# A decoder layer on one core: a fourth pair of weight blocks by seven products of quarters

## The chip, the core and the metric

The kernel runs on one core of a Trainium2 chip. The core's engines run their own instruction streams beside each other and wait for one another by semaphores: PE (TensorE, matrix products into PSUM), DVE (VectorE), ACT (ScalarE), POOL (GpSimd) and SP (SyncE, which here only starts transfers). Data lie in HBM, and are brought to the core's SBUF by DMA queues; SP's queue and POOL's queue are the two that matter. The metric is the device time of one execution in microseconds (us). The time before is the median of three runs, 1008.59 us (1008.1 to 1008.62).

## The reference, cut to what matters

A decoder layer on 256 tokens of width 2048 with two parallel mixers, all in float32:

```
proj = x @ w_in              # q_lat 4096 | c_kv | attn_gate 2048 | indexer | x_rnn 2048 | rnn_gate 2048 | g_a 2048 | g_b 2048
attn = sparse_attention(q_lat, c_kv, ...)                 # 16 heads, top-64 keys
branch_a = (attn * silu(attn_gate)) @ w_branch_a          # 2048 x 2048
h = rglru(x_rnn, ...)       # conv, gates r and i; a = exp(-8 r softplus), b = sqrt(1 - a^2) (i xc); h_t = a h_(t-1) + b
branch_b = (h * silu(rnn_gate)) @ w_branch_b              # 2048 x 2048
merged = sigmoid(g_a) * branch_a + sigmoid(g_b) * branch_b
out = layernorm(2 ** 0.25 * x + merged @ w_out)
```

The change touches how g_a (its first 1024 columns) is computed and when the exponentials and roots of the recurrence are done.

## The kernel before

**Products.** Every float32 value is split into a high and a low part: `hi_of` (L146, ACT) copies the rounded high part, `lo_of` (L150, DVE) subtracts it from the value. A product is three matmuls: high with high, high with low, low with high. The tokens `xs` stay in SBUF in this form. The weights stream: `load_to` has SP fetch pieces of 512 KB into four `raw` buffers, `split_to` turns each into one of five `hi` and five `lo` buffers, and PE uses them. The list `halves` fixes the order of all pieces. `split_to(n + 5)` and `load_to(n + 9)` at the point where PE uses piece n say how far ahead ACT, DVE and SP have been programmed; a buffer is written only when PE (or DVE, for `raw`) is through with what was in it.

**Jobs.** `col_jobs` lists the work in order: qi, the attention gate ag, the latent queries q with the heads beside them, then ga0, ga1, the four blocks of branch A ba0 to ba3, then xr (input of the recurrence), gb1, gb2, rg (its gate), and a tail of branch B and the output product, whose order is a table, and a layer norm. The column tiles of w_in (qi, ag, q, xr, rg) take weights as the stationary operand and are called pairs, in `pair` (two tiles of 128 columns at a time, 32 matmuls of 512 columns and 32 of 256; L384). The blocks of 512 columns (ga, ba, gb, bb) are **chunks**: eight pieces, sixteen ticks, each tick six matmuls 128x512 (two token halves times three, L1310 to L1312), 96 in all.

**Seven products.** Where two blocks multiply the same tokens, their two times two quarters can be had from seven products of quarters in place of eight, with sums of token quarters and of weight quarters. This is done for three pairs: ga2 with gb3 (steps j1 to j4, during q), ga3 with gb0 (steps s1 and s2, `seven_step`, during ba1 to ba3) and bb0 with bb1 (steps t1 to t3, in the tail). The sums of weights for j and s are formed by DVE just before the split; those for t are built in HBM scratch ahead of time by `weight_sums`: SP copies one quarter, POOL starts an accumulating transfer of the other (`add_rows`, L270). The token sums for j are built once during q (`early_sums`, `late_sum`), those for s once more by `quarter_sums`, with loads of x, DVE sums (L990 to L993) and splits, from the start of ga0. An s2 step takes two pieces: one of 1024 columns and one of 512, whose sum (`form`, L368) DVE forms first, and nine matmuls.

**Everything else** hangs on ticks. `spawn(t, generator)` puts a piece of work into an agenda, and `tick(t)` runs each up to its next yield, so a tick decides where in the engines' queues an instruction stands. `D0`, `C0` and `G0` are the ticks where q, xr and the first gb after xr begin. The recurrence: for each of 16 tiles n, `decay(n)` does tanh and exp on ACT (L896, L897), a square on POOL (L900) and a combination on DVE (L902), one tile every four thirds of a tick from G0 + 14; `roots(q)` takes the square roots of four tiles at a time on ACT (L906), G0 + 37 and 38; `post_rg` follows each tile of rg with the eviction (L467, L471), the gate (L920), the scan (L922) and the split of the result.

Of the kernel before, what the change touches and what calls it, by code (L numbers as in the profile page):

```python
# [18 lines left out]
P = 128  # L19
# [35 lines left out]
def col_jobs():  # L55
# [26 lines left out]
YAT = 66  # L82
NAT = 74
# [17 lines left out]
OPERANDS = {"t1a": ("11", "t1"), "t1b": ("t2", "t3"), "t2": ("21", "t4")}  # L101
# [17 lines left out]
def layer(ctx, tc, ar, out):  # L119
# [87 lines left out]
    relb = const.tile([P, P], F32, name="relb")  # L207
# [9 lines left out]
    for job in jobs:  # L217
# [1449 lines left out]
```

## Time and profile before

| what | before |
|---|---|
| median of three runs | 1008.59 us (1008.1 to 1008.62) |
| the profiled execution's own time | 1009.1 us |
| its span, first to last instruction | 1007.3 us |
| mean granted TensorE clock | 0.998 |
| busy: PE / DVE / ACT / POOL | 999.9 / 811.2 / 613.7 / 161.7 us |
| moved by DMA | 233.17 MB, 231 GB/s in the mean |

How to read it: the span is taken from one profiled execution, and 1.8 us of its time lie around it. Busy times are per engine; the engines run beside each other. A row such as `L150 DVE TENSOR_TENSOR lo<-raw,hi 128x1024 ... x360 | 429.2, 1201 | 154.0 <-ACT hi L146 150.2` says: line 150, on DVE, output lo from raw and hi, partitions by elements, 360 of them, 429.2 us busy in all, 1201 ns the mean of one, the engine idle for 154.0 us just before them, of which 150.2 ended when ACT's hi of line 146 was done. In a timeline a row begins with its start and its duration, and a bracket gives idle time before it. In the table by windows each row gives, for a stretch of the span, its length, the busy time and count on each engine, the clock, the share of the DMA engines' time and the rate.

### The profile page before, as it was taken

The page shows a single profiled execution, that of the slowest core. Times are in us where ns is not written, and L with a number is a line of the kernel's source. Part 1 is how long each engine was busy: PE and PEld are TensorE (multiplying, and loading weights), DVE is VectorE, ACT ScalarE, POOL GpSimd, SP SyncE. Part 2 cuts the span into 40 slices and gives each one's busy share as a digit, 9 for nine tenths or more (in the row PEclk, how much of TensorE's full clock was granted, in tenths as well). Part 3 has the DMA queues.
Part 4 walks back from the last instruction along what each step waited for, and adds up shares of the span by engine and source line. Part 5 has one row for each costly group of instructions (what it writes and reads, how often), then busy time and mean ns, then how long its engine had stood idle before and what let it go on. Part 6 is the DMA issues. An engine that isn't in the chain of part 4 may idle for free.

```text
span 1007.3 us, 15201 instructions
## 1 busy us (share of the span) xinstructions
PE 999.9 (99%) x5296; PEld 862.3 (86%) x5296; DVE 811.2 (81%) x1333; ACT 613.7 (61%) x1043; POOL 161.7 (16%) x194
## 2 busy tenths in 40 slices
PE   9999999999999999999999999999999999999997
PEld 8888888888888888888888888888888888888885
DVE  5678789878789988868888868888669898788587
ACT  5576656666776576576555555555886557665452
POOL 0015621111123311210000000000253320000002
PEclk9999999999999999999999999999999999999999
DMA  9846886766656665788988778888786657888952
GB/s 304 263 146 200 273 317 210 236 222 199 189 157 209 198 195 172 232 248 259 280 268 278 225 243 241 275 238 266 223 234 191 202 171 258 271 282 291 325 185 84
DMA packets 77133, 233.17 MB, mean 231 GB/s; under 512 B 8176, under 2 KB 15216, under 8 KB 75776
## 3 DMA queue, kind: packets, MB, share of 16 engines
q1 hardware_dynamic: 71488, 214.20, 64.6%
q0 software_dynamic: 4848, 17.07, 7.4%
q8 instruction: 42, 0.69, 0.3%
q10 hardware_dynamic: 720, 0.92, 0.3%
q14 instruction: 35, 0.29, 0.1%
HBM read 230.03 MB, written 23.10 MB: 251 GB/s over the span
## 4 chain that ended last, share of the span: by engine, by line
PE 99%; DVE 0%; DVEq 0%; issue 0%
PE ps_q L384 18%; PE ps_ag L384 9%; PE ps_rg L384 9%; PE ps_xr L384 9%; PE ps_ba L1311 3%; PE ps_ba L1312 3%; PE ps_ba L1310 3%; PE psq L384 2%; PE ps_qi L384 2%; PE ps_o L1209 2%; PE ps_o L1206 2%; PE ps_o L1207 2%; PE ps_bb L1206 2%; PE ps_bb L1209 2%; PE ps_bb L1207 2%; PE ps_ga L1310 1%
## 5 line engine op out<-in xcount | busy, mean ns | idle before, releaser
L150 DVE TENSOR_TENSOR lo<-raw,hi 128x1024 fp32r<-128x1024 f32 (+1 forms) x360 | 429.2, 1201 | 154.0 <-ACT hi L146 150.2
L146 ACT ACTIVATE hi<-raw 128x1024 fp32r<-128x1024 f32 (+1 forms) x360 | 360.7, 1018 | 146.1 <-PE ps_q L384 16.8
L384 PE MATMUL ps_q<-xs,hi 128*128 128x512 f32 x512 | 126.9, 391 | 0.0
L384 PEld LDWEIGHTS ps_q<-xs,hi 128*128 128x128 f32 x512 | 94.0, 188 | 18.4
L384 PEld LDWEIGHTS ps_q<-xs,lo 128*128 128x128 f32 x512 | 65.6, 191 | 2.5
L384 PE MATMUL ps_q<-xs,lo 128*128 128x256 f32 x512 | 66.4, 283 | 0.0
L641 POOL TENSOR_TENSOR bias<-bias,mask 128x256 f32<-128x256 f32 (+1 forms) x32 | 32.7, 1041 | 194.3 <-DMA bias<-dz 156.6
L384 PE MATMUL ps_ag<-xs,hi 128*128 128x512 f32 x256 | 60.1, 391 | 0.0
L384 PE MATMUL ps_rg<-xs,hi 128*128 128x512 f32 x256 | 59.5, 390 | 0.0
L384 PE MATMUL ps_xr<-xs,hi 128*128 128x512 f32 x256 | 59.5, 390 | 0.0
L384 PEld LDWEIGHTS ps_xr<-xs,hi 128*128 128x128 f32 x256 | 47.6, 188 | 9.6
L384 PEld LDWEIGHTS ps_rg<-xs,hi 128*128 128x128 f32 x256 | 47.6, 188 | 9.6
L384 PEld LDWEIGHTS ps_ag<-xs,hi 128*128 128x128 f32 x256 | 47.5, 188 | 9.6
L1312 PE MATMUL ps_ba<-hi,ua 128*128 128x512 f32 x128 | 49.8, 389 | 0.0
L1311 PE MATMUL ps_ba<-lo,ua 128*128 128x512 f32 x128 | 49.8, 389 | 0.0
L1310 PE MATMUL ps_ba<-hi,ua 128*128 128x512 f32 x128 | 49.8, 389 | 0.0
L146 ACT ACTIVATE hi<-form 128x512 fp32r<-128x512 f32 x40 | 25.3, 633 | 28.4 <-PE ps_ba L1312 8.7
L1206 PE MATMUL ps_o<-hi,xs 128*128 128x512 f32 x96 | 37.6, 392 | 0.0
L1209 PE MATMUL ps_o<-hi,xs 128*128 128x512 f32 x96 | 37.4, 390 | 0.0
L1207 PE MATMUL ps_o<-lo,xs 128*128 128x512 f32 x96 | 37.4, 389 | 0.0
L384 PE MATMUL ps_ag<-xs,lo 128*128 128x256 f32 x256 | 32.9, 283 | 0.0
L384 PE MATMUL ps_xr<-xs,lo 128*128 128x256 f32 x256 | 32.8, 282 | 0.0
(439 smaller groups left out, 2166.3 us busy)
## 6 DMA issues: line engine op xcount, KB each, us to landing
raw<-in_wt SPq DMA_DIRECT2D x168, 512.0 KB, 4.9
raw<-in_wba SPq DMA_DIRECT2D x32, 512.0 KB, 4.9
raw<-in_wo SPq DMA_DIRECT2D x32, 512.0 KB, 4.6
raw<-in_wga SPq DMA_DIRECT2D x24, 512.0 KB, 4.8
raw<-in_wgb SPq DMA_DIRECT2D x20, 512.0 KB, 5.1
raw<-in_wbb SPq DMA_DIRECT2D x20, 512.0 KB, 4.5
sum_t<-in_wbp SPq DMA_DIRECT2D x16, 512.0 KB, 6.6
raw<-in_ws SPq DMA_DIRECT2D x16, 512.0 KB, 4.7
```

What stands on the lines that cost most here:

```text
L146: nc.scalar.activation(hi, src, AF.Copy)
L150: nc.vector.tensor_sub(lo, src, f(hi))
L384: nc.tensor.matmul(ps[:, :n], w, rhs[:, :n], start=start, stop=stop)
L641: nc.gpsimd.tensor_add(b[:, r, :W[r]], b[:, r, :W[r]], mask[:, r, :W[r]])
L1206: nc.tensor.matmul(o, mh, hi, start=left[t] == left_of[key][t], stop=False)
L1207: nc.tensor.matmul(o, mh, lo, start=False, stop=False)
L1209: nc.tensor.matmul(o, ml, hi, start=False, stop=left[t] == 0)
L1310: nc.tensor.matmul(o, mh, hi, start=first and d == 0, stop=False)
L1311: nc.tensor.matmul(o, mh, lo, start=False, stop=False)
L1312: nc.tensor.matmul(o, ml, hi, start=False, stop=d == KT - 1)
```

## The change

- **A fourth pair.** ga0 and ga1 are no longer chunks. They are computed as the quarters of one product in four kinds of steps, r1 (8 steps), r2 (4), r3 (8), r4 (8), each with one piece and six matmuls 128x512 (`r_step`, L1185 to L1187 after the change), 168 matmuls where there were 192. Their results are combined by `after_r1` to `after_r4`.
- **Its weight sums** are built in HBM scratch like those of t, by the same `weight_sums`, now with a set, from tick 4 on, every 11 ticks with pauses (16 copies by SP, 16 accumulating transfers by POOL).
- **Token sums are stored and fetched again.** `early_sums` and `late_sum` store what they built for j to HBM scratch `kept` (SP, in the q stage). `load_sums`, from the start of gb1, fetches it by 16 transfers on POOL's queue into buffers that the last heads give back; the r and s steps read them. `quarter_sums` is gone. Signs of sums are changed so that the same token sums serve all three pairs.
- **Order.** gb1 moves from behind xr to ahead of the ba chunks; the ba chunks come in the order 2, 0, 1, 3. The table `EXTRAS` says which steps stand ahead of which piece of which chunk. In s2, six steps now stand in a row ahead of the last piece of ba3, where steps and pieces alternated.
- **The recurrence.** tanh is done with each tile's gates in xr. `decays` does eight tiles at once: 0 to 7 at C0 + 50, 8 to 15 at G0 + 17, with the first roots at G0 + 18 and the rest at G0 + 34. Only one chunk, gb2, is left between xr and rg. `lru_consts` comes earlier, and the buffer for `decay` is allocated at C0 and later holds y.

PE, in the middle of the first chunk after q, between heads 13 and 14 of the attention (`ps_ga0_0` and `ps_ga0_1` are the two token halves of ga0; hi and lo are the split pieces by number). Before:

```order
L1310 MATMUL ps_ga0_0_4881<-hi138_4830,xs_93 128x512
L1311 MATMUL ps_ga0_0_4881<-lo138_4831,xs_93 128x512
L1312 MATMUL ps_ga0_0_4881<-hi138_4830,xs_93 128x512
L1310 MATMUL ps_ga0_1_4882<-hi138_4830,xs_93 128x512
L1311 MATMUL ps_ga0_1_4882<-lo138_4831,xs_93 128x512
L1312 MATMUL ps_ga0_1_4882<-hi138_4830,xs_93 128x512
```

The same place after the change (`psr_1` and `psr_2` are two of the seven products, `ps_gb1_0` a token half of gb1):

```order
L1185 MATMUL psr_1_5080<-hi138_4939,xs_93 128x512
L1186 MATMUL psr_1_5080<-lo138_4940,xs_93 128x512
L1187 MATMUL psr_1_5080<-hi138_4939,xs_93 128x512
L1185 MATMUL psr_2_5081<-hi138_4939,xs_93 128x512
L1186 MATMUL psr_2_5081<-lo138_4940,xs_93 128x512
L1187 MATMUL psr_2_5081<-hi138_4939,xs_93 128x512
L1185 MATMUL psr_1_5080<-hi139_4971,xs_93 128x512
L1186 MATMUL psr_1_5080<-lo139_4972,xs_93 128x512
L1187 MATMUL psr_1_5080<-hi139_4971,xs_93 128x512
L1428 MATMUL ps_gb1_0_4989<-hi140_4983,xs_93 128x512
```

A chunk's piece is used for twelve matmuls, a step's piece for six, so the pieces follow each other faster where steps stand.

ACT, where rg begins (`gb2` is evicted, `ri` and `decay` belong to the recurrence, hi268 and hi280 are pieces of rg). Before:

```order
L772 ACTIVATE gb2_0_7998<-ps_gb2_0_7768 128x512
L146 ACTIVATE hi268_8000<-raw268_7894 128x1024
L772 ACTIVATE gb2_1_8017<-ps_gb2_1_7769 128x512
L896 ACTIVATE decay_7743<-ri15_7710,c8_91 128x256
L897 ACTIVATE ri15_7710<-ri15_7710,nc8_92 128x256
L906 ACT_TABLE_LOAD
L906 ACTIVATE decay_7743<-decay_7743 128x1024 x2
L146 ACTIVATE hi269_8059<-raw269_7918 128x1024
L906 ACTIVATE decay_7743<-decay_7743 128x1024 x2
```

After:

```order
L174 ACTIVATE hi280_8093<-raw280_7989 128x1024
L944 ACT_TABLE_LOAD
L944 ACTIVATE ri8_7623<-ri8_7623,nc8_92 128x256
L944 ACTIVATE ri9_7640<-ri9_7640,nc8_92 128x256
L944 ACTIVATE ri10_7792<-ri10_7792,nc8_92 128x256
L944 ACTIVATE ri11_7806<-ri11_7806,nc8_92 128x256
L944 ACTIVATE ri12_7928<-ri12_7928,nc8_92 128x256
L944 ACTIVATE ri13_7946<-ri13_7946,nc8_92 128x256
L944 ACTIVATE ri14_8028<-ri14_8028,nc8_92 128x256
L944 ACTIVATE ri15_8061<-ri15_8061,nc8_92 128x256
L958 ACT_TABLE_LOAD
L958 ACTIVATE decay_6725<-decay_6725 128x1024 x2
```

Eight exponentials, two loads of tables and two roots now stand between two splits; before, the exponentials were spread over the gb chunks.

DVE, behind that place, after the change (a2 are the squares that POOL made, lo280 to lo284 the low parts of rg's pieces, s_rg the evicted tile):

```order
L178 TENSOR_TENSOR lo280_8094<-raw280_7989,hi280_8093 128x1024
L960 MEMSET decay_6725 128x4 x2
L954 SCALAR_TENSOR_TENSOR decay_6725<-a28_8128,decay_6725 128x256
L954 SCALAR_TENSOR_TENSOR decay_6725<-a29_8140,decay_6725 128x256
L954 SCALAR_TENSOR_TENSOR decay_6725<-a210_8152,decay_6725 128x256
L178 TENSOR_TENSOR lo281_8168<-raw281_8007,hi281_8167 128x1024
L954 SCALAR_TENSOR_TENSOR decay_6725<-a211_8164,decay_6725 128x256
L178 TENSOR_TENSOR lo282_8188<-raw282_8035,hi282_8187 128x1024
L954 SCALAR_TENSOR_TENSOR decay_6725<-a212_8182,decay_6725 128x256
L510 TENSOR_TENSOR s_rg0_8205<-ps_rg0_8080,r_rg0_8185 128x256
L178 TENSOR_TENSOR lo283_8208<-raw283_8069,hi283_8207 128x1024
L954 SCALAR_TENSOR_TENSOR decay_6725<-a213_8202,decay_6725 128x256
```

Before, the combinations (L902) were all ahead of rg's second tile; now eight stand among its low parts.

The diff, cut to its core:

```diff
-    jobs += [("ga", i) for i in range(2)] + [("ba", i) for i in range(4)]
+    jobs += [("gb", 1)] + [("ba", i) for i in (2, 0, 1, 3)]
     jobs += [("xr", i) for i in range(16)]
-    jobs += [("gb", i) for i in range(1, 3)] + [("rg", i) for i in range(16)]
+    jobs += [("gb", 2)] + [("rg", i) for i in range(16)]
...
-    return {("ba", 1): ("s1", (0, None, 1, None, 2, None, 3, None)),
-            ("ba", 2): ("s1", (4, None, 5, None, 6, None, 7, None)),
-            ("ba", 3): ("s2", tuple(range(8)))}.get(job)
+    return EXTRAS.get(job, ((),) * 8)
...
+RAT = 4
+RGAP = 11
+RPAUSE = {1: 6, 2: 6, 3: 6, 4: 6, 5: 6, 6: 48}
...
+    ("gb", 1): ((), (), R1[0:2], R1[2:4], (), (), R1[4:7], ()),
+    ("ba", 2): ((), R1[7:8], R3[0:1], R3[1:4], R3[4:5], (), R3[5:8], ()),
+    ("ba", 0): (R4[0:3], R4[3:8], (), (), R2[0:2], R2[2:4] + S1[0:1], S1[1:2], ()),
+    ("ba", 1): (S1[2:3], S1[3:4], (), (), (), (), (), S1[4:5]),
+    ("ba", 3): (S1[5:6], S1[6:7], S1[7:8], (), (), S2[0:1], S2[1:2], S2[2:8]),
...
-    def decay(n):
-        r, w = ri[n][:, :T], v[:, n, :]
-        nc.scalar.activation(w, r, AF.Tanh, scale=c8[:, n:n + 1])
-        nc.scalar.activation(r, r, AF.Exp, scale=nc8[:, n:n + 1])
...
+    def decays(ns):
+        for n in ns:
+            nc.scalar.activation(ri[n][:, :T], ri[n][:, :T], AF.Exp, scale=nc8[:, n:n + 1])
...
+    def load_sums():
...
+            for s, d in zip((2, 3, 1, 4), dst):
+                nc.gpsimd.dma_start(f(d), kept[s, j])
...
+    def r_step(phase, k):
+        i = where[phase, k]
+        split_to(i + 5)
+        load_to(i + 9)
...
+        todo = {"r1": lambda: ((1, a(k, 0)), (2, a(8 + k, 0))),
+                "r2": lambda: ((4, a(8 + 2 * k, 1)), (4, a(9 + 2 * k, 1))),
+                "r3": lambda: ((6, S[2, k]), (7, S[3, k])),
+                "r4": lambda: ((5, S[1, k]), (3, S[4, k]))}[phase]()
...
+            nc.tensor.matmul(psr[p], mh, hi, start=first, stop=False)
+            nc.tensor.matmul(psr[p], mh, lo, start=False, stop=False)
+            nc.tensor.matmul(psr[p], ml, hi, start=False, stop=last)
+        parts.pop(i)
+        split_to(i + 6)
+        load_to(i + 10)
...
-    spawn(C0 + WAT, weight_sums(WGAP))
+    spawn(C0 + WAT, weight_sums("t", WGAP, {}))
+    spawn(RAT, weight_sums("r", RGAP, RPAUSE))
...
-    spawn(at["ga", 0] + 2, quarter_sums())
+    spawn(at["gb", 1] + SAT, load_sums())
...
-    for n in range(16):
-        spawn(G0 + 14 + 4 * n // 3, decay(n))
+    spawn(C0 + DEC, decays(range(8)))
+    spawn(G0 + DEC2, decays(range(8, 16)))
     for q in range(4):
-        spawn(G0 + 37 + q // 2, roots(q))
+        spawn(G0 + (DEC2 + 1, DEC2 + 1, ROOTS, ROOTS)[q], roots(q))
```

More of the change, by code (lines that the diff above doesn't have):

```diff
@@ L113, in ticks @@
 def ticks(job):
-    return 16 if job[0] in CHUNKS else 4
+    if job[0] not in CHUNKS:
+        return 4
+    return 16 + sum(phase[0] == "r" for steps in seven(job) for phase, _ in steps)
 @with_exitstack
@@ L153, in layer @@
     accs, auxs = [0, 1, 2, 3], [4, 5, 6, 7]
+    order = list(range(8))
     def bank(n, name):
+        n = order[n]
         return psum.tile([P, 512], F32, name=name, tag=f"bank{n}", bufs=1)
@@ L221, in layer @@
         for pc in range(8 if job[0] in CHUNKS else 2):
-            step = seven(job) and (seven(job)[0], seven(job)[1][pc])
-            if step and step[1] is not None:
+            for step in seven(job)[pc] if job[0] in CHUNKS else ():
                 where[step] = len(halves)
-                halves += [(step[0] + e, step[1], 0) for e in "ab"]
+                halves += [(step[0] + e, step[1], 0) for e in ("ab" if step[0][0] == "s" else ("",))]
             where[job, pc] = len(halves)
@@ L298, in load_to @@
                 src = ar["ws"][a + (8 if kind == "s2a" else 0)].rearrange("p k c -> p (k c)")
+            elif kind == "r2":
+                for e in range(2):
+                    nc.sync.dma_start(raw[:, e * 512:(e + 1) * 512], quarter("r", "t4", 2 * a + e))
+                continue
             elif kind == "t3":
@@ L770, in post_gb @@
         for t in range(2):
-            g = gates["gb", i, t] = gate_tile(f"gb{i}_{t}", "form")
+            if i == 1:
+                g = att.tile([P, 512], F32, name=f"gbt{t}", tag="gbt", bufs=2)
+            else:
+                g = gate_tile(f"gb{i}_{t}", "form")
+            gates["gb", i, t] = g
             nc.scalar.activation(g, pss[t], AF.Copy)
             yield
+    done = set()
     def post_ba(i, pss):
         for t in range(2):
+            assert i == 3 or (i, t) in done, (i, t)
             g = gates["ga", i, t]
@@ L956, in layer, with load_quarters @@
     S = {}
-    def load_quarters(n):
-        x = [gate_tile(f"form{n}_{j}", "form") for j in range(8)]
+    def load_quarters():
+        x = [gate_tile(f"form0_{j}", "form") for j in range(8)]
         form.update(enumerate(x))
@@ L1026, in early_sums @@
                     SJ[s, 2 * j + e] = (homes[s, j][:, e, 0, :], homes[s, j][:, e, 1, :])
+        yield KEEP
+        for j in range(4):
+            for s in v:
+                nc.sync.dma_start(kept[s, j], f(homes[s, j]).rearrange("p k e t -> p (k e t)"))
+                yield 2
     def late_sum(j):
@@ L1046, in late_sum @@
             SJ[3, 2 * j + i] = (hi[:, i, :], lo[:, i, :])
+        yield 3
+        for e, part in enumerate((hi, lo)):
+            nc.sync.dma_start(kept[3, j][:, e * T:(e + 1) * T], f(part).rearrange("p k t -> p (k t)"))
     psj = {}
@@ L1113, in layer, with after_r2 @@
+    def after_r2():
+        nc.vector.tensor_add(cr["c"], psr[4], cr["c"])
+        accs.insert(1, 3)
+        auxs.append(7)
+        yield
+        for e, n in enumerate("bcad"):
+            nc.scalar.activation(cr[n], cr[n], AF.Sigmoid)
+            done.add(divmod(e, 2))
+            yield
+    after_r = {("r1", 7): after_r1, ("r2", 3): after_r2, ("r3", 7): after_r3, ("r4", 7): after_r4}
     ps7 = {}
@@ L1165, in after_s2 @@
             nc.scalar.activation(g, v, AF.Sigmoid)
+        yield
+        for t in range(2):
+            g = gate_tile(f"gb1_{t}", "form")
+            nc.scalar.activation(g, gates["gb", 1, t], AF.Copy)
+            gates["gb", 1, t] = g
     SB = {}
```

216 lines of the change are left out of this document (137 added, 79 removed).

## The prediction

> **What bounds the kernel now.** I read the page's first two parts, then the waits of PE, then the chain.
>
> ```profile
> PE 999.9 (99%) x5296; PEld 862.3 (86%) x5296; DVE 811.2 (81%) x1333; ACT 613.7 (61%) x1043; POOL 161.7 (16%) x194
> DMA  9846886766656665788988778888786657888952
> GB/s 304 263 146 200 273 317 210 236 222 199 189 157 209 198 195 172 232 248 259 280 268 278 225 243 241 275 238 266 223 234 191 202 171 258 271 282 291 325 185 84
> PE 99%; DVE 0%; DVEq 0%; issue 0%
> ...
> PE warm L397 <- DVE eps L200: 1.0, 1, 1.0
> PE psn L1537 <- ACT mrow L146: 0.4, 1, 0.4
> PE pm L1534 <- DVE mcol L1531: 0.3, 1, 0.3
> ```
>
> The span is 1007.3 us, PE is busy for 999.9 of it, and its three waits together are 1.7 us: one at the start, two in the layer norm at the end. So between them nothing is waited for, and the time is the number of PE instructions times what each takes. A microsecond less on PE is a microsecond less in all, as long as the split pieces (ACT's high part, DVE's low part) and the transfers stay ahead. VectorE at 81% and transfers at eight tenths say that the reserve is not large; so I price PE first and then look for the places where the change eats the reserve.
>
> **What leaves PE.** Gates ga0 and ga1 were two chunks of 96 matmuls. Now they are 28 steps r1 to r4 of 6 matmuls, 168, all of the same shape 128x512.
>
> ```profile
> L1310 PE MATMUL ps_ga<-hi,xs 128*128 128x512 f32 x64 | 25.3, 395 | 0.0
> L1311 PE MATMUL ps_ga<-lo,xs 128*128 128x512 f32 x64 | 24.9, 389 | 0.0
> L1312 PE MATMUL ps_ga<-hi,xs 128*128 128x512 f32 x64 | 25.0, 390 | 0.0
> ...
> core 0: us, PE busy (x) PEld busy (x) DVE busy (x) ACT busy (x) POOL busy (x), PEclk, DMA share, GB/s
> 466.33:488.09 21.76, 21.76 (x97) 18.02 (x96) 18.80 (x29) 12.32 (x19) 1.03 (x1) 1.00 0.93 279
> ```
>
> The three rows are the 192 matmuls of ga0 and ga1. Their 390 ns is the length of one, and neighbours overlap, so the cost of one more or less is read from a stretch of nothing else: chunk ba0, alone from 466.33 to 488.09, is 96 matmuls in 21.76 us at full clock, 0.2267 us each. 24 fewer are **5.44 us** less. Every other product remains: gb1, the ba chunks and s1, s2 are moved and not lengthened, and sign changes turn a subtraction into an addition of the same shape.
>
> The Trainium skill ("TensorE: Matmul & The Clock Gate", section Back-to-back issue gap) gives 131 ns for one in a sustained stream of 512 columns, and 216 ns for an isolated one; by the first the 24 would be worth 3.1 us and the time 1005.8, by the second 5.2 us and 1003.8. The window above shows 226.7 ns in a stream, so neither holds here and the trace's figure is taken.
>
> **What is added beside PE.** Splitting 28 pieces in place of 16 adds 12 times 1.20 us on DVE and 12 times 1.02 us on ACT. Against that go the second set of token sums:
>
> ```profile
> L150 DVE TENSOR_TENSOR lo<-raw,hi 128x1024 fp32r<-128x1024 f32 (+1 forms) x360 | 429.2, 1201 | 154.0 <-ACT hi L146 150.2
> L146 ACT ACTIVATE hi<-raw 128x1024 fp32r<-128x1024 f32 (+1 forms) x360 | 360.7, 1018 | 146.1 <-PE ps_q L384 16.8
> L990 DVE TENSOR_TENSOR sum<-form,form x4: 416/418/421, 445.1 to 472.1; 128x256 f32<-128x256 f32 x4
> form<-in_xT POOLq DMA_DIRECT2D x16, 256.0 KB, 6.2
> ```
>
> L990 (shortest, median and longest in ns) is one of four such lines, 16 sums of 0.42 us with 16 low parts as short (13 us), and 16 high parts on ACT. DVE so gains about 14.4 + 7 combinations of 0.69 us (the form sum's row, below) - 13 = 6 us over a stage of 109 us, ACT about 6: both have more idle than that in the stage (DVE's busy share in ba0 is 18.80 of 21.76, so 15 us per 109). In the mean it is hidden.
>
> The sums come back by 16 transfers of 256 KB on POOL's queue. A row of the same size and queue takes 6.2 us to land. The last group may start only once head 15 (pspv15) is through; r3's fifth and seventh step, the first to read groups that wait so, come 54 and 90 matmuls behind it, 12 and 20 us. That is twice the landing: cost 0, and 3 us at most, if two groups queued one behind the other (2 x 6.2 plus some 2 us of POOL's issues, less 12). Behind the waiting POOL instruction stand only the sums for the tail, needed 250 us later. The 16 copies and 16 accumulating transfers of the weight sums start at tick 4 and are spread over the ag and q stages, where the slices show 146 to 236 GB/s; POOL waits there for copies that are three gaps of 11 ticks old: 0.
>
> **Three places where the reserve could run out.**
>
> (a) Transfers, from gb1 to the end of ba0. PE has 480 matmuls there, 108.8 us. To be moved: 52 pieces of 0.524 MB, two s1 steps of 0.786, 16 returning sums of 0.262, five copies and two accumulations of 0.524 for the tail's sums, one bias: 36.9 MB. Nine pieces (4 raw, 5 split) are there beforehand, 4.7 MB, so 32.2 MB in 108.8 us, **296 GB/s**.
>
> ```profile
> 480.00:520.00 40.00, 40.00 (x178) 33.14 (x177) 34.60 (x42) 20.64 (x24) 3.02 (x3) 1.00 0.89 269
> 120.00:135.00 15.00, 15.00 (x85) 13.18 (x84) 12.75 (x40) 9.37 (x13) 8.36 (x13) 1.00 1.02 385
> 900.00:945.00 45.00, 45.00 (x211) 37.15 (x210) 35.71 (x38) 24.91 (x27) 0.00 (x0) 1.00 0.89 312
> 735.61:746.72 11.11, 11.11 (x66) 9.86 (x65) 6.01 (x9) 9.86 (x14) 4.04 (x5) 1.00 1.02 286
> ```
>
> The last two columns are the share of the 16 engines and the rate. 312 GB/s ran for 45 us at 0.89, 385 for 15 us; but the stretch with accumulating transfers (480 to 520) has 269 at the same 0.89, which is 302 at full share, and one short stretch was full at 286. All four ran without a wait of PE. 296 lies inside; I take 0, with 0 to 13 us as ends (36.9 MB at 302 with no lead is 122 us, for 108.8). At 286 it would be 112.6, a stall of 3.8.
>
> (b) Six steps of s2 in a row at the end of ba3, where before a step and a chunk piece took turns.
>
> ```profile
> L368 DVE TENSOR_TENSOR form<-form,raw 128x512 f32<-128x512 f32 x8 | 5.5, 686 | 0.1
> L150 DVE TENSOR_TENSOR lo<-form,hi 128x512 fp32r<-128x512 f32 x40 | 27.9, 698 | 0.1
> 563.21 0.63 ACT L146 ACTIVATE hi<-form 128x512 fp32r<-128x512 f32 x1 [1.39 <-PE ps_ba L1312]
> ```
>
> A step needs 0.69 + 1.20 + 0.70 = 2.59 us of DVE and 9 matmuls, 2.04 us, of PE. Six in a row leave DVE 3.3 us behind. The last row, from the same stage, shows ACT waiting for PE to free a buffer, so the lead of five buffers is full, two and a half steps or 6.5 us of DVE's work: 0 taken, 0 to 3.3 as ends. Behind the run come pairs of xr, which use fewer pieces per microsecond, and the lead is built again.
>
> (c) The start of rg. Two tables are loaded, eight exponentials and two roots done by ACT in one burst between two splits.
>
> ```profile
> L897 ACT ACTIVATE ri<-ri,nc 128x256 f32<-128x256 f32 x16 | 8.2, 511 | 0.5
> 735.61 88.88 PE ps_rg L384 x512
> 737.33 1.05 ACT L146 ACTIVATE hi<-raw 128x1024 fp32r<-128x1024 f32 x1
> 739.82 1.28 ACT L906 ACT_TABLE_LOAD   x1
> 741.11 2.01 ACT L906 ACTIVATE decay<-decay 128x1024 f32<-128x1024 f32 x2
> 748.48 1.59 DVE L150 TENSOR_TENSOR lo<-raw,hi 128x1024 fp32r<-128x1024 f32 x1 [1.86 <-ACT hi L146]
> 753.20 1.34 DVE L150 TENSOR_TENSOR lo<-raw,hi 128x1024 fp32r<-128x1024 f32 x1 [1.05 <-ACT hi L146]
> 754.91 0.42 ACT L920 ACTIVATE g<-s_rg 128x256 f32<-128x256 f32 x1 [1.74 <-DVE s_rg L471]
> 756.92 1.04 ACT L146 ACTIVATE hi<-raw 128x1024 fp32r<-128x1024 f32 x1
> L902 DVE SCALAR_TENSOR_TENSOR decay<-a,decay 128x256 f32<-128x256 f32 x16 | 8.4, 550 | 0.5 <-POOL a L900 0.5
> ```
>
> The burst is 2 x 1.28 + 8 x 0.51 + 2.01 = 8.7 us. The split before it ended 2.8 us into rg (737.33 + 1.05 - 735.61), so the next ends at 2.8 + 8.7 + 1.06 = 12.5. Two tiles of rg take 88.88/8 = 11.11 us on PE; the buffer that this split writes is freed at 8.3 (four high parts, 7.3, and one low part, 0.95), and PE wants it at 11.11 + 1.83 = 12.94. It is 0.4 us early, by a clock that can be wrong by as much. After that eight combinations of 0.55, 4.4 us, stand between the low parts on DVE, whose idle time there is 1.86 + 1.05 = 2.9; they slip by 1.5, ACT's gate (754.91, waiting for DVE) with them, and the split behind it, which ended at 757.96 and was wanted at 735.61 + 22.22 + 1.83 = 759.66, 1.7 before. Again nearly nothing is left. I take **0.4 us** lost, with 0 and 2.7 as ends (burst and slip each late by their own length over the lead, plus a landing that was waited for 1.15 us). The other eight exponentials, done in one burst during xr, fall where the buffers are full: 0, up to 1.
>
> The Trainium skill ("ScalarE: Activation LUTs", section What ACT_TABLE_LOAD costs) has a drain of 1.38 us behind each load. Here the next instruction starts 0.01 us after the load's end (739.82 + 1.28, 741.11), so the trace disagrees.
>
> **Sum.** On the profiled execution, 1007.3 and 1.8 around it, 1009.1: 1009.1 - 5.44 + 0.4 = 1004.1. The median of the runs shown is 0.5 lower, 1008.59, and gives **1003.5**.
>
> **Rivals.** *The reserve runs out in part*: the burst of (c), the run of (b) or the transfers of (a) at 286 cost 1 to 4 us; 1004.5 to 1006.6. For it: (c) has half a microsecond left by its own working. Against it: PE never waited in places as dense.
> *The drain counts*: each of the two loads holds ACT 1.4 us more, by (c) nearly all of it is late, and PE waits 2.4 us more: 1005.9. The two rows speak against it. It is inside the first rival's range, and I give it 0.03 of its chance. The drain is the rule of the Trainium skill named above ("ScalarE: Activation LUTs").
> *The transfers bound the r stage*: from gb1 to ba0 the rate stays at 302 and the lead was not full, so PE waits 13.4 us, net 8 slower, 1016.6. It decides from 282 GB/s on: there the stall, 32.2 MB in 114.2 us, eats the 5.44; below 277 the kernel is slower by more than 0.2%. For it: 302 at full share with accumulating transfers. Against: 312 and 385 without.
> *The gain is eaten*: (a) and (c) together cost 3.5 to 7.5, within 0.2% of before.
> *The change does not do what it says*: the instructions are counted, 24 fewer on PE, so only if the order made PE wait as much; that is the case just named.
>
> **Chances.** Clean (1002.8 to 1004.3) 0.60; partly run out (to 1006.6) 0.20; within 0.2%, 2.0 us, about what a measurement of this kernel can tell from no change, 0.12; slower 0.08. The range of 8 in 10 leaves out 0.03 below and most of the last two cases: 1002.5 to 1007.0, its upper end being a stall of 3.5 us, in the middle of the ends of (a) to (c).
>
> **What would show it.** PE's instructions fall by 24 and its busy time by 5.4; its list of waits stays at the three rows (clean), or gains one: on ACT's hi or DVE's lo in the second or third pair of rg for (c), in ps (s2) at the end of ba3 for (b), on a transfer (raw or kept) or on hi behind raw between gb1 and ba0 for (a). The rate in that stage should be near 296 (36.9 MB over a somewhat longer stretch when the lead is rebuilt). ACT should show the burst as one row of 8 x 0.51 with the splits late behind it. Wrong would be: waits of PE over 4 us in sum, or matmuls that take other than 0.2267 us beside the denser transfers.

## The result, and the profile after

The changed kernel took 1022.65 us (median of four runs, 1019.25 to 1024.12) against 1008.61 us for the kernel before on the same chip (1008.1 to 1009.16): 1.0134 times the time before, 95% interval 1.0109 to 1.0160. It is 14 us slower, where 5 less were forecast. The profiled execution, the shortest of the four, took 1019.25 us with a span of 1017.4. That is 10.1 us above the profiled execution before, and these are accounted for below; the three longer runs left no trace.

After the change, the page's busy times, transfers by slice and chain, then the list of PE's waits (total, times, longest):

```profile
PE 999.8 (98%) x5272; PEld 858.2 (84%) x5272; DVE 819.8 (81%) x1320; ACT 625.8 (62%) x1046; POOL 182.1 (18%) x218
...
DMA  8759998899868978888998777887858658888952
...
PE 82%; DMA 6%; DVE 5%; ACT 5%; issue 2%; SPq 0%; DVEq 0%; ACTq 0%
...
PE ps_rg L423 <- ACT hi L174: 4.1, 2, 3.7
PE psr L1185 <- issue: 1.6, 1, 1.6
PE psj L1119 <- DVE gb L1147: 1.2, 1, 1.2
PE ps_ba L1429 <- DVE lo L178: 1.2, 1, 1.2
PE ps_ba L1428 <- ACT gbt L815: 1.1, 1, 1.1
```

PE has its 24 instructions less, but the chain, which was PE for 99%, is PE for 82%: it now runs through transfers, DVE and ACT. The three waits of before were 1.7 us; the five new ones shown are 9.2 us, and one loss cannot be seen in this list, a slower clock behind the longest of them (below).

Where the time went is read from the first and last starts of PE's instructions on one tile. Before, then after (shortest, median and longest in ns, then first and last start):

```profile
L1310 PE MATMUL ps_ga<-hi,xs x64: 389/389/481, 416.8 to 465.6; 128*128 128x512 f32 x64
L384 PE MATMUL ps_xr<-xs,hi x256: 388/389/398, 591.6 to 683.5; 128*128 128x512 f32 x128
L384 PE MATMUL ps_rg<-xs,hi x256: 389/389/398, 735.5 to 820.3; 128*128 128x512 f32 x128
```

```profile
L1428 PE MATMUL ps_gb<-hi,xs x64: 389/389/481, 418.8 to 738.3; 128*128 128x512 f32 x64
L423 PE MATMUL ps_xr<-xs,hi x256: 388/389/398, 616.3 to 708.2; 128*128 128x512 f32 x128
L423 PE MATMUL ps_rg<-xs,hi x256: 387/389/628, 738.9 to 830.1; 128*128 128x512 f32 x128
```

From the first chunk behind q to xr (the **r stage**) it was 174.8 us, is 197.5, and should be 191.1: 72 matmuls more stand there (gb1 came, 24 went), 16.3 us. rg's first to last start grew from 84.8 to 91.2, and up to the tail's first matmul from 88.8 to 95.3. In this way each stage of each profile was set against its count of matmuls; us lost, with the medians:

| run | median us | ratio to before, interval | q | r stage | xr | gb2 | rg | start of tail |
|---|---|---|---|---|---|---|---|---|
| the change | 1022.65 | 1.0134 [1.0109, 1.0160] | 1.7 | 6.4 | 0.1 | 0.4 | 6.5 | -0.1 |
| e1_roots | 1015.44 | 1.0067 [1.0052, 1.0082] | 0.9 | 8.7 | 0.1 | 1.6 | 0.1 | 0.0 |
| e2_tsums | 1015.55 | 1.0071 [1.0050, 1.0093] | 1.0 | 1.2 | 0.1 | 0.0 | 4.5 | 0.7 |
| e3_spread | 1024.05 | 1.0147 [1.0128, 1.0165] | 1.5 | 12.1 | 0.1 | 2.1 | 6.1 | -0.1 |
| e4_all | 1012.69 | 1.0041 [1.0025, 1.0058] | 1.5 | 1.7 | 0.0 | 1.7 | 0.9 | 2.8 |
| e5_memset | 1020.32 | 1.0110 [1.0095, 1.0125] | 1.7 | 9.1 | 0.1 | 1.2 | 5.0 | 0.4 |
| e6_nokept | 1016.86 | 1.0083 [1.0068, 1.0098] | 2.1 | 7.2 | 0.1 | 1.4 | 6.0 | 0.0 |
| e7_noaccum | 1012.78 | 1.0036 [1.0022, 1.0050] | 2.3 | 3.9 | 0.0 | 0.0 | 3.0 | 0.4 |
| e8_norsums | 1020.27 | 1.0118 [1.0097, 1.0139] | 0.2 | 8.7 | 0.1 | 0.2 | 7.6 | 0.0 |
| e9_raw5 | 1012.93 | 1.0044 [1.0029, 1.0059] | 1.2 | 1.2 | 0.1 | 0.1 | 5.9 | -0.1 |
| e10_best | 1016.02 | 1.0080 [1.0066, 1.0093] | 1.0 | 3.2 | 4.6 | 4.3 | 0.1 | 0.0 |
| e11_best_s | 1019.72 | 1.0102 [1.0089, 1.0115] | 1.7 | 6.4 | 4.6 | 4.0 | 0.1 | 0.5 |
| e12_queues | 1020.36 | 1.0113 [1.0097, 1.0129] | 1.5 | 8.2 | 0.1 | 1.5 | 5.3 | 0.4 |
| e13_queues_t | 1020.33 | 1.0106 [1.0092, 1.0120] | 1.5 | 4.4 | 0.1 | 0.0 | 6.0 | 4.4 |
| e14_queues_t_r | 1023.89 | 1.0150 [1.0122, 1.0177] | 5.0 | 4.5 | 0.1 | -0.1 | 8.6 | 2.8 |
| e15_roots_t6 | 1010.33 | 1.0020 [1.0010, 1.0030] | 1.2 | 4.7 | 0.2 | 3.1 | 0.1 | 0.0 |
| e16_roots_t | 1013.64 | 1.0045 [1.0031, 1.0060] | 1.6 | 1.9 | 0.1 | 1.6 | 1.3 | 4.4 |

(start of the tail: first matmul of bb2 to first of bb3). For the change the losses come to 15.0, with 0.3 at the kernel's start 15.3; less the 5.44 that left PE, 9.9 of the 10.1 us. A kernel that waits varies more from run to run than the one before; the columns come from one execution each, so a microsecond there, or two in the medians, says little, and a tenth is rounding. Two profiles lie far from their medians: e2's is its shortest run of ten (1011.05 of 1011.05 to 1020.62), e15's one of its longer ones (1012.98).

Part of some columns is a stretch in which PE ran at half its clock (last section), 1.7 us each: in rg of the change, e2, e3, e5, e6, e9 and e13 (2.6 and 2.8 in e8 and e14), in the r stage of e3, e11, e13 and e14, in gb2 of e10, xr of e11, q of e14 and the tail of e13 and e16.

How the r stage waits is seen at the first r4 step. ACT and DVE after the change (start, duration, in brackets the idle time before and what ended it):

```profile
487.07 1.06 ACT L174 ACTIVATE hi<-raw 128x1024 fp32r<-128x1024 f32 x1 [3.02 <-DMA raw<-in_wga]
...
490.32 1.06 ACT L174 ACTIVATE hi<-raw 128x1024 fp32r<-128x1024 f32 x1 [0.72 <-DMA raw<-in_wga]
...
491.41 1.23 DVE L178 TENSOR_TENSOR lo<-raw,hi 128x1024 fp32r<-128x1024 f32 x1 [0.55 <-ACT hi L174]
492.55 0.68 DVE L1201 TENSOR_TENSOR ga<-psr,ga 128x512 f32<-128x512 f32 x1
```

A piece lands late, ACT's high part waits for it, DVE's low part for that, and behind the low part in DVE's queue stands the combination that empties the PSUM bank (L1201, done at 493.23). r4's first matmul, which needs that bank, started at 493.3, 1.8 us late; the list of waits calls it "issue". The wait for `gbt` is the same by way of ACT: the eviction of gb1 stood in its queue behind a split whose piece was late.

At the start of rg, ACT, DVE and POOL after the change, and two windows (PE busy first, then clock):

```profile
744.80 3.31 ACT L944 ACTIVATE ri<-ri,nc 128x256 f32<-128x256 f32 x8
...
749.40 2.01 ACT L958 ACTIVATE decay<-decay 128x1024 f32<-128x1024 f32 x2
...
750.53 0.06 DVE L960 MEMSET decay<- 128x4 f32 x1 [5.79 <-ACT decay L958]
751.46 0.42 DVE L954 SCALAR_TENSOR_TENSOR decay<-a,decay 128x256 f32<-128x256 f32 x1 [0.86 <-POOL decay L966]
...
755.14 0.95 DVE L954 SCALAR_TENSOR_TENSOR decay<-a,decay 128x256 f32<-128x256 f32 x1
756.01 1.63 DVE L178 TENSOR_TENSOR lo<-raw,hi 128x1024 fp32r<-128x1024 f32 x1
...
756.52 1.72 POOL L966 TENSOR_TENSOR decay<-decay,ri 128x256 f32<-128x256 f32 x1
...
764.16 0.42 ACT L972 ACTIVATE g<-s_rg 128x256 f32<-128x256 f32 x1 [3.64 <-DVE s_rg L510]
...
766.48 1.04 ACT L174 ACTIVATE hi<-raw 128x1024 fp32r<-128x1024 f32 x1
...
763.40:767.70 4.30, 0.57 (x3) 0.15 (x3) 4.01 (x8) 1.96 (x4) 4.02 (x6) 1.00 0.39 138
767.70:771.60 3.90, 3.90 (x11) 3.05 (x12) 3.61 (x5) 2.82 (x6) 0.53 (x2) 0.56 0.94 170
```

DVE stands still for 5.8 us behind a memset that waits for ACT's roots. Then the combinations come together with POOL's products, and both get slow: 0.95 us beside POOL where one alone took 0.42, a low part 1.63 for 1.23. The second tile's gate on ACT (764.16) waits 3.6 us for DVE, the split behind it (766.48) ends 22.7 us after the first exponential, PE waits 4.1 us from start to start, and runs at 0.56 of its clock, in the mean, for the 3.9 us after that. The burst of exponentials and roots also began late: the first exponential stood 5.9 us into rg, and 1.25 us of that was ACT's wait for a piece of rg to land.

### The profile page after: what moved, and what is told of

The parts are those of the page before. It is cut to its first block, busy times and chain, and to the rows that moved or that the text cites. A ratio compares the mean times of both kernels' runs of the same rounds, so it can differ in the third digit from the quotient of the medians.

```text
span 1017.4 us, 15291 instructions
## 1 busy us (share of the span) xinstructions
PE 999.8 (98%) x5272; PEld 858.2 (84%) x5272; DVE 819.8 (81%) x1320; ACT 625.8 (62%) x1046; POOL 182.1 (18%) x218
## 4 chain that ended last, share of the span: by engine, by line
PE 82%; DMA 6%; DVE 5%; ACT 5%; issue 2%; SPq 0%; DVEq 0%; ACTq 0%
PE ps_q L423 18%; PE ps_ag L423 9%; PE ps_rg L423 7%; PE ps_xr L423 6%; ACT hi L174 2%; DVE lo L178 2%; PE psq L423 2%; PE ps_qi L423 2%; PE ps_o L1323 2%; PE ps_o L1326 2%; PE ps_o L1324 2%; PE ps_bb L1324 2%; PE ps_bb L1323 2%; PE ps_bb L1326 2%; PE ps_ba L1429 2%; PE ps_ba L1428 2%
## 5 line engine op out<-in xcount | busy, mean ns | idle before, releaser
L178 DVE TENSOR_TENSOR lo<-raw,hi 128x1024 fp32r<-128x1024 f32 (+1 forms) x372 | 441.2, 1196 | 141.6 <-ACT hi L174 138.6
L174 ACT ACTIVATE hi<-raw 128x1024 fp32r<-128x1024 f32 (+1 forms) x372 | 374.2, 1020 | 177.0 <-DMA raw<-in_wt 17.4
L423 PE MATMUL ps_rg<-xs,hi 128*128 128x512 f32 x256 | 61.8, 398 | 4.1 <-ACT hi L174 4.1
```

Of the source, the lines that this page charges most:

```text
L174: nc.scalar.activation(hi, src, AF.Copy)
L178: nc.vector.tensor_sub(lo, src, f(hi))
L423: nc.tensor.matmul(ps[:, :n], w, rhs[:, :n], start=start, stop=stop)
```

## The experiments

All are the changed kernel but for the edit shown, timed against the kernel before. e6 to e9 leave out work that the result needs, and serve for the times alone.

**e1_roots.** The first eight tiles' roots into xr.

```diff
-        spawn(G0 + (DEC2 + 1, DEC2 + 1, ROOTS, ROOTS)[q], roots(q))
+        spawn((C0 + DEC + 10, C0 + DEC + 10, G0 + ROOTS, G0 + ROOTS)[q], roots(q))
```

> The first eight tiles' roots are taken in xr (C0 + 60) in place of the start of rg; nothing else moves. Theory rg-burst (the DVE's memset that waits for the roots holds up eight combinations, and these then run beside POOL's squares and slip behind the splits): the two waits of PE in rg (0.8 and 4.1 us from start to start) and the slow matmuls behind the longer one go, rg takes 89 to 90 us in place of 95.3, and the time falls by 4 to 7 us. Rival (the exponentials and table loads alone make hi late, or the transfers of rg do): rg stays at 93 us or more, time falls by less than 2 us.

Measured: 1015.44 us, 7 below the change; rg lost 0.1 in place of 6.5. PE's row, DVE's behind the eight exponentials, then ACT's:

```profile
L423 PE MATMUL ps_rg<-xs,hi x256: 389/389/398, 740.4 to 825.3; 128*128 128x512 f32 x128
...
746.69 1.16 DVE L954 SCALAR_TENSOR_TENSOR decay<-a,decay 128x256 f32<-128x256 f32 x2 [1.35 <-POOL a L951]
...
749.68 1.33 DVE L178 TENSOR_TENSOR lo<-raw,hi 128x1024 fp32r<-128x1024 f32 x1 [0.51 <-ACT hi L174]
...
745.39 3.31 ACT L944 ACTIVATE ri<-ri,nc 128x256 f32<-128x256 f32 x8
...
761.03 1.05 ACT L174 ACTIVATE hi<-raw 128x1024 fp32r<-128x1024 f32 x1
```

The matmuls run from 740.4 to 825.3, 84.9 us as before the change, and none is over 398 ns. From the first exponential to the end of the split behind the second gate (761.03; the **rg path** below) it is now 16.7 us; in the change, and in the six other runs that leave rg alone (e2, e3, e6 to e9), it is 22.7 to 22.8. So what rg lost came from the roots' place in the burst, and they are worth 6.0 us of that path. With the roots went ACT's 3.3 us for them, the memsets behind them and four products of POOL (L966); what part is whose, this run does not say. gb2, which now follows the roots closely, lost 1.6.

**e2_tsums, e3_spread.** The tail's sums later; the same r steps spread more evenly.

```diff
-WAT = -84
-WGAP = 11
+WAT = 4
+WGAP = 7
```

> The tail's weight sums are built from xr on (16 copies, 16 accumulations, every 7 ticks) in place of from the middle of ba2 on; rg's burst stays. Theory transfers (the stretch from gb1 to ba1 moves too much, so raw pieces land late): with 5 MB less in it, the 6.4 us lost between gb1 and xr shrink to 2 to 4, the time falls by 2 to 4 us, and the waits of ACT for raw pieces there get shorter. Rival crowding (four raw buffers and a landing of 5 us limit the steps in bursts, whatever else is moved): the loss there stays at 5 to 6.5 us. A cost is possible in xr or rg, where the copies go now: up to 2 us.

```diff
-    ("gb", 1): ((), (), R1[0:2], R1[2:4], (), (), R1[4:7], ()),
-    ("ba", 2): ((), R1[7:8], R3[0:1], R3[1:4], R3[4:5], (), R3[5:8], ()),
-    ("ba", 0): (R4[0:3], R4[3:8], (), (), R2[0:2], R2[2:4] + S1[0:1], S1[1:2], ()),
+    ("gb", 1): ((), (), R1[0:2], R1[2:3], R1[3:4], R1[4:5], R1[5:7], ()),
+    ("ba", 2): ((), R1[7:8], R3[0:1], R3[1:3], R3[3:5], R3[5:6], R3[6:8], ()),
+    ("ba", 0): (R4[0:2], R4[2:5], R4[5:8], (), R2[0:2], R2[2:4] + S1[0:1], S1[1:2], ()),
```

> The same steps, spread more evenly: r3 1-2-2-1-2 in place of 1-3-1-0-3, r4 2-3-3 in place of 3-5. Theory crowding: the loss between gb1 and xr shrinks from 6.4 to 2 to 4 us, time lower by 2 to 4 us. Theory transfers (bytes of the whole stretch): the loss stays at 5 to 6.5 us, as the bytes are the same.

Measured: e2 1015.55, the r stage lost 1.2 in place of 6.4; e3 1024.05, the r stage lost 12.1. Spreading the steps inside their chunks helped nothing: the r4 steps still stand in the first half of ba0, so the pieces needed there are the same. Taking the tail's transfers out of the stage helped: e2's 1.2 is from its shortest run, but the other four runs with its `WAT` lost 1.7, 1.9, 4.4 and 4.5 there (e4, e16, e13, e14; 1.7 of each of the last two is half clock), against 6.4 to 12.1 where these sums were built at their old place (the change, e1, e3, e5, e8, e12).

**e4_all.** The three edits together.

> All three moves together. If their causes are separate the gains add: rg 89 to 90 us, the loss between gb1 and xr under 2 us, time 1004 to 1010. If a shared limit stands behind both (transfers everywhere), the sum stays above 1014.

Measured: 1012.69. Both losses went (1.7 and 0.9), but gb2 lost 1.7 and the tail's start 2.8, by one wait:

```profile
PE ps_bb L1324 <- DVE lo L178: 2.5, 1, 2.5
```

The gains of e1 and e2 are 14.3 us together, and e3 cost 1.4; 10 were had.

**e5_memset.** DVE's memset ahead of the root.

```diff
-        nc.scalar.activation(w, w, AF.Sqrt)
-        yield
         nc.vector.memset(w[:, :, 0:1], 1.0)
+        nc.scalar.activation(w, w, AF.Sqrt)
+        yield
```

> In roots the memset of the first token's column stands ahead of the root (the root of 1 is 1) in place of behind it; so DVE's queue no longer waits for ACT's roots at the start of rg. Roots, exponentials and POOL's products stay where the change put them. Theory queue (DVE stood still 5.8 us behind that memset with eight combinations ready behind it): rg takes 89 to 91 us in place of 95.3, the time falls by 4 to 6 us. Rival port (the combinations are slow because POOL runs beside DVE, 0.95 us in place of 0.42) or rival burst (ACT's exponentials, roots and table loads): rg stays at 93 us or more, the time falls by less than 2.

Measured: 1020.32, rg lost 5.0. Here is why so little; DVE, then POOL:

```profile
747.43 1.16 DVE L954 SCALAR_TENSOR_TENSOR decay<-a,decay 128x256 f32<-128x256 f32 x2 [1.33 <-POOL a L951]
753.24 0.95 DVE L954 SCALAR_TENSOR_TENSOR decay<-a,decay 128x256 f32<-128x256 f32 x1 [4.65 <-POOL a L951]
...
751.89 0.74 POOL L966 TENSOR_TENSOR decay<-decay,ri 128x256 f32<-128x256 f32 x1 [3.92 <-ACT decay L959]
```

DVE got past the memset, did two combinations, and then waited 4.65 us for a square that stood in POOL's queue behind a product that needs ACT's roots. The wait had moved to another queue: the rg path took 21.9 us here, 0.8 less than in the change.

**e6_nokept, e7_noaccum.** Without the fetch of the stored sums; without the accumulating transfers of the tail's sums.

```diff
-                nc.gpsimd.dma_start(f(d), kept[s, j])
...
+                    S[s, 2 * j + k] = [xs[:, 2 * j + k, s // 3 * P:s // 3 * P + P], xs[:, 2 * j + k, T:T + P]]
```

> The 16 transfers that bring the stored token sums back (4.2 MB on POOL's queue, in gb1 and ba2) are left out; the r and s steps read slices of xs in their place. Theory bytes (the stretch from gb1 to xr carries too many bytes, of whatever kind): 4.2 MB less bring about what e2's 5 MB less brought, the loss there shrinks from 6.4 to 1.5 to 3 us and the time falls by 4 to 7. Rival (it is the tail's copies and accumulations that hurt, by reading and writing HBM at once): the loss shrinks by 2 us at most, as these still run from ba2 on.

```diff
-                if len(begun) > 2:
+                if len(begun) > 2 and set == "r":
...
-        while begun:
+        while begun and set == "r":
```

> The 16 accumulating transfers of the tail's weight sums are left out, their 16 copies stay at their places. Theory bytes: of what the tail's sums move in the stretch the accumulations are about a third by count (two or three of seven or eight), so the loss there shrinks by 1 to 2.5 us. Theory accumulation (these are what slows the other transfers): it shrinks by 4 us or more, to about what e2 left. Theory copies: no change, within 1 us.

Measured: e6 1016.86, but its profile shows 7.2 lost in the r stage, no better than the change; this one is inconclusive, its median speaking for the theory of bytes and its profile (1019.28, its longest run) against. e7 1012.78, with 3.9 lost there: by these single profiles the accumulations are about half of what e2 removed. e7 also lost only 3.0 in rg. Its rg path took 22.8 us, as in the change, but it began 3.3 us into rg in place of 5.9, and no stretch of half clock followed; so when the burst begins, and with it the landing that ACT waits for ahead of it, is part of rg's loss. The other runs bear this out: the first exponential 4.0 us into rg goes with 4.5 lost (e2), 5.3 with 5.9 (e9), 6.3 with 7.6 (e8).

**e8_norsums.** Without the fourth pair's weight sums.

```diff
-    spawn(RAT, weight_sums("r", RGAP, RPAUSE))
```

> The weight sums of the fourth pair (16 copies, 16 accumulations in the ag and q stages) are left out, the r steps read plain quarters in their place. Theory traffic: the stretch from q to gb1 goes back from 257.7 to 256.0 us and the wait of psj for DVE's gb (1.2 us) goes; the time falls by 1 to 2 us. Rival (kept stores or the changed order in the queues): it stays at 257 to 258 us.

Measured: 1020.27; q lost 0.2 in place of 1.7, and the wait of psj (PE's products of the j steps) for `gb` was gone from the list. So the loss in q came from these sums (the sixteen profiles with them lost 0.9 to 5.0 there).

**e9_raw5.** As e6, with a fifth raw buffer up to the last r step, and loads begun one piece earlier.

```diff
+            if lo5 <= i < hi5 and (i - lo5) % 5 == 0:
+                raw = att.tile([P, 1024], F32, name=f"raw{i}", tag="rawx", bufs=1)
```

> As e6_nokept (the stored sums are not fetched, slices of xs are read), and in the buffers that this frees a fifth raw buffer for the pieces from gb1 to the last r step, with loads started one piece earlier; s, xr and rg have four as before. Theory landing (in the r steps a piece is used every 1.36 us, and four buffers with 5 us to land, 1.06 and 1.2 us to split can bring one only every 1.9 or so): the 7 us lost between gb1 and xr in e6 shrink to 2 to 4, the time falls by 3 to 5 below e6's 1016.9. Theory rate (the DMA engines have no more to give): nothing changes, within 1.5 us, and the landings get longer instead.

Measured: 1012.93, 4 below e6; the r stage lost 1.2 in place of 7.2. Windows of about the same work in ba2, ba0 and ba1, and the median landing (from issue to arrival) of the 512 KB pieces of ba in them, for the change, e2, e6 and e9 (the last three columns are clock, share of the DMA engines, GB/s):

```profile
490.00:543.00 53.00, 49.84 (x214) 39.45 (x213) 43.33 (x49) 30.02 (x34) 3.09 (x3) 1.00 0.96 305
raw<-in_wba SPq DMA_DIRECT2D x11, 512.0 KB, 5.5
```

```profile
487.00:537.00 50.00, 50.00 (x221) 41.12 (x220) 42.40 (x49) 28.84 (x33) 0.00 (x0) 1.00 0.78 257
raw<-in_wba SPq DMA_DIRECT2D x11, 512.0 KB, 4.3
```

```profile
489.00:542.00 53.00, 47.98 (x205) 37.71 (x205) 41.52 (x48) 28.61 (x33) 3.09 (x3) 1.00 0.94 299
raw<-in_wba SPq DMA_DIRECT2D x11, 512.0 KB, 5.1
```

```profile
487.00:535.00 48.00, 48.00 (x212) 39.31 (x211) 39.24 (x45) 27.38 (x32) 3.09 (x3) 1.00 0.98 319
raw<-in_wba SPq DMA_DIRECT2D x10, 512.0 KB, 5.8
```

This tells the two theories apart. e9 fetches what e6 fetches; it moved more per second (319 GB/s for 299, and 305 in the change), at longer landings, and PE did not wait; so in e6 and in the change the rate was not at its end, though a share of 0.98 leaves little beyond e9. e2 had the landing down to 4.3 us and PE did not wait either. What bounds the stage is the ring of buffers: each is held for 5.5 us to land and 1.06 and 1.2 to split, so four give a piece every 1.94 us (7.8 / 4). By the same sum it is 1.84 in e6, 1.64 in e2, and 1.61 in e9 with five. In the first half of ba0 the eight r4 steps and four pieces of the chunk are 12 pieces for 96 matmuls, one per 1.81 us of PE's time. This is an estimate from medians, and e6 lies close to the line, but it parts the two that wait from the two that do not: either a shorter landing or one buffer more ends the wait.

**e10_best, e11_best_s.** Two tries to have both gains: the first eight tiles' exponentials and roots earlier in xr (DEC 46, roots 10 ticks later), the tail's sums from ba1 on (`WAT = -30`, `WGAP = 8`); then also s1's steps out of ba0.

```diff
-    ("ba", 1): (S1[2:3], S1[3:4], (), (), (), (), (), S1[4:5]),
+    ("ba", 1): (S1[0:1], (), S1[1:2], (), S1[2:3], (), S1[3:4], S1[4:5]),
```

> The change with the first eight tiles' exponentials and roots taken earlier in xr (C0 + 46 and C0 + 56, clear of gb2) and the tail's sums built from ba1's start on (C0 - 30, every 8 ticks). If the two causes are the whole of it: rg 89 us, gb1 to xr 192 to 193 (2 lost), gb2 25, q 257.5: time 1004 to 1007, below before by 0.2 to 0.4%. If they only move the waits on, as e4 did to the tail: 1009 to 1013.

> As e10_best, and the s1 steps leave ba0 (where r4, r2 and s1 stood together) and alternate with ba1's pieces. Theory crowding of ba0: what is still lost there (3 us in e2) goes to 1 or less, the time is 1 to 3 us below e10. Rival (ba1 has no room, DVE is busy 0.86 there): the loss moves to ba1 and ba3, the time is that of e10 within 1 us or above it.

Measured: 1016.02 and 1019.72. rg was clean in both, but xr lost 4.6 and gb2 4. For xr this points to the burst's place more than to the copies: e15 has denser copies in xr, with the burst four ticks later, and lost 0.2 there. What gb2 lost was not taken apart. Moving s1 brought nothing (r stage 6.4, of which 1.7 is half clock, for 3.2).

**e12_queues, e13_queues_t, e14_queues_t_r.** POOL's four products moved back as well; with e2's sums; and with the fourth pair's sums 6 ticks apart.

```diff
+        nc.vector.memset(w[:, :, 0:1], 1.0)
         nc.scalar.activation(w, w, AF.Sqrt)
-        yield
-        nc.vector.memset(w[:, :, 0:1], 1.0)
+        yield 4 if q == 0 else 1
```

> As e5_memset, and POOL's first four products with the roots stand four ticks later in its queue, behind five of the eight squares; so neither DVE's queue nor POOL's waits for ACT's roots before squares and combinations are done. Exponentials and roots stay where the change put them. Theory queues (in e5 the wait went from DVE's queue to POOL's, 3.9 us for the roots ahead of a product, and DVE's combinations waited 4.65 us for a square behind it): rg takes 89 to 91 us in place of 93.8, time 4 to 6 us below the change's 1022.7. Rival burst (ACT's 8.7 us between two splits are the limit): rg stays at 93 or more.

> e12's order in rg and e2's place for the tail's sums together. If rg and the stretch from gb1 to xr were the two large losses, the gains add: 1007 to 1010, with 1 to 1.5 us left in q, 1 in gb1 to xr and 1 in the tail. If moving the tail's sums takes from rg or the tail what it gave before (as in e4): 1011 or more.

> As e13, and the fourth pair's weight sums 6 ticks apart in place of 11 after their pause, done by the middle of q. Theory traffic in q (e8: without these sums q took 256.2 in place of 257.7 us): they are through before the wait of psj at 358 us, which goes; time 0.5 to 1.5 us below e13. Rival (denser transfers make a new wait earlier in q): the same or slower than e13.

Measured: 1020.36, 1020.33 and 1023.89; rg lost 5.3, 6.0 and 8.6. The queues alone are not enough. DVE, then ACT, in e12:

```profile
754.66 1.23 DVE L178 TENSOR_TENSOR lo<-raw,hi 128x1024 fp32r<-128x1024 f32 x1 [3.83 <-ACT hi L174]
...
763.11 0.96 DVE L954 SCALAR_TENSOR_TENSOR decay<-a,decay 128x256 f32<-128x256 f32 x1
...
747.05 3.31 ACT L944 ACTIVATE ri<-ri,nc 128x256 f32<-128x256 f32 x8
...
767.31 1.04 ACT L174 ACTIVATE hi<-raw 128x1024 fp32r<-128x1024 f32 x1
...
776.09 2.01 ACT L959 ACTIVATE decay<-decay 128x1024 f32<-128x1024 f32 x2 [1.25 <-DVE decay L958]
```

With both queues free, DVE waited 3.8 us for ACT itself, whose next split came after the roots, and the last combinations still ran late and beside POOL. The rg path took 21.3 us: e12's order took off 1.4 of the 6.0 that the roots are worth. The edit also brought a wait of its own: at the second pair of roots ACT waits for the memset now ahead of them (the last row), and PE waits 1.7 us from start to start behind it. Of the four orders tried, only the shorter burst (e1, without the roots and their table load, 3.3 us, and without POOL's four products) cured rg. In e14 the denser sums cost 5.0 us in q, 1.7 of it half clock, so closer spacing is no cure; wider spacing was not tried.

**e15_roots_t6, e16_roots_t.** e1's roots with the tail's sums done before rg (`WAT = -30`, `WGAP = 6`), and with e2's.

> e1's roots in xr and the tail's sums from ba1's start on, six ticks apart, so that they are done before rg. If e4's tail loss (2.8 us) came from the sums' transfers beside rg: the tail takes 30.2 us again, and with rg at 89 and gb1 to xr at 192 to 193 the time is 1007 to 1009, level with before. If denser transfers in ba1, ba3 and xr make waits there: 1010 to 1014.

> e1's roots and e2's sums, with the change's own order of the steps (e4 without e3). If e3's order was harmful there too: gb1 to xr at 192 as in e2, the time 1 to 2 us below e4's 1012.7. If not: 1012 to 1014.

Measured: 1010.33 (1.0020 [1.0010, 1.0030], twelve runs) and 1013.64. e15 is the best that was found, 12 us below the change and still not below the kernel before: its profiled run, 2.7 above its median, loses 4.7 in the r stage, 3.1 in gb2 and 1.2 in q, 9.0 for the 5.44 gained. No version beat the kernel before.

## Why the prediction was wrong

- **What leaves PE**: right. 24 instructions left, and stages without waits keep their length per matmul (xr took 97.36 us before and after).
- **"In the mean it is hidden", cost 0**: right for DVE and ACT in busy time, and no use: no stage was lost for lack of their mean.
- **The transfers that the change adds**: "0" for the weight sums in ag and q was wrong, 1.5 us by e8; by what path they reach PE was not followed. For the fetched sums, e6 leaves it open.
- **(a), the r stage**: here the first step failed. The prediction set bytes against a rate, "296 lies inside; I take 0". The rate was 305 GB/s and there was still a wait, and 319 in e9 without one. The quantity that mattered was not in the working: a buffer's turn. Four pieces of 0.524 MB per 5.5 + 1.06 + 1.2 = 7.8 us are 270 GB/s for the split pieces alone, and the tail's copies and accumulations raised the landing from 4.3 (e2) to 5.5 us. In the mean that would have done, as 52 pieces in 108.8 us are 250 GB/s; the first half of ba0 needs 289, which a mean over the stage does not show. The loss of 6.4 lay within the ends 0 to 13, but the value was taken at the lower end. The rival "the transfers bound the r stage" had place and sign; its threshold of 282 GB/s was of the wrong kind.
- **(b), six s2 steps in a row**: right, ba3 lost nothing (43.7 us from its first matmul to xr, 192 matmuls of 0.2267 are 43.5).
- **(c), the start of rg**: the place and the mechanism were right, the term was mis-sized, 0.4 for 6.5 us, and the end of 2.7 too. The 0.4 itself was no result of the working, which had the split 0.4 us early, but an allowance for error. The burst took no longer than was worked out (743.50 to 751.41, 7.9 us for 8.7). Missed were four things that the rows show: the split before the burst ended 4.5 us into rg where 2.8 was set, behind a wait of 1.25 for a landing that the working had only in its upper end; DVE's and POOL's queues stood still behind the roots, so that eight combinations were not spread over the idle time but came at once; beside POOL each took 0.95 us in place of 0.55, so they slipped by more than the 1.7 us of lead; and the wait that followed brought the clock down, another 1.7 us. e1 shows that the roots in the burst decide, worth 6.0 us of the rg path; e5 and e12 that the queues alone are 0.8 to 1.4 of it. How the rest divides between ACT's 3.3 us for the roots and POOL's products beside DVE was not tested.
- **The rival "the drain counts"** did not occur: in e1 the first exponential began 0.02 us after the load's end (744.09 + 1.28, 745.39).
- **The chances**: "PE never waited in places as dense" was taken as evidence of reserve. It was evidence only for the landings of before; 8% for slower was far too little with three places at half a microsecond to nothing of margin.

Left open: why the median of the change is 3 us above its profiled run (its clock, 0.997 there and 0.995 or 0.996 in the other three, would fit about one more stretch of half clock, 1.7 us, an estimate; the rest is unknown); what e6 removed; and what makes ba2's wait for `gbt` vary, from 0.4 us in e2 to 2.4 in e10.

## What to carry to other kernels

Where a ring of buffers feeds the engine that bounds, compare the pieces needed per microsecond, in the most crowded stretch and not in the mean, with buffers divided by landing plus processing time, with the landing that the added traffic will cause; the bytes against the best rate seen are not enough. Where work that was spread out is gathered into one burst on an in-order engine, follow each queue that needs its result and see what then runs at the same time; a saving on the bounding engine that is smaller than the lead it uses up is not a saving.

## What the hardware showed

Behind a wait of PE of 4.1 us, from one matmul's start to the next, the granted clock was 0.56 in the mean of 3.9 us (the window above): it was exactly half from 768.07 to 771.48 us, 3.41 us, and full on both sides, and matmuls of 512 columns came 0.43 us apart there. The profiles of the changed kernels hold 18 such stretches inside the run, 16 of 3.41 us and two twice as long (e8, e14). One of 3.41 us costs 1.7 us on top of the wait, which a sum of waits does not show.

Every wait of 3.0 us or more, from start to start, brought one. Of shorter waits some did: 2.9 us in e2, 2.5 in e10, 2.4 in e13, 2.2 in e11. Others as long did not: 2.9 in e4, 2.8 in e10, 2.7 in e12, 2.2 in e5. What decides between them no run shows. e12, e2 and e11 behind such waits:

```profile
768.40:771.00 2.60, 2.60 (x11) 2.16 (x12) 2.30 (x2) 2.42 (x4) 0.61 (x1) 1.00 0.95 151
```

```profile
762.00:766.00 4.00, 4.00 (x16) 3.22 (x15) 4.00 (x5) 3.78 (x5) 2.21 (x2) 0.81 0.94 281
```

```profile
458.50:461.80 3.30, 3.30 (x9) 2.60 (x8) 1.80 (x2) 1.06 (x1) 0.00 (x0) 0.50 0.66 212
```

The Trainium skill ("TensorE: Matmul & The Clock Gate", section What's actually happening) has the clock fall to half after an idle window of about 3.4 us. The 4.1 us of the change and the 2.7 of e12 agree with that; the 2.2 to 2.9 us of e2, e10, e11 and e13 are shorter and were enough.

DVE's combinations took 0.42 us alone and 0.95 beside POOL, its low parts 1.23 and 1.63, POOL's products 0.74 and 1.72. The Trainium skill ("SBUF — State Buffer", section SBUF: two separate sides) says that a DVE operation with two inputs in SBUF and a GpSimd operation take turns at a shared port; the sign agrees, and it is a rule against gathering this work that the prediction did not weigh.
